# Corner of a triangular inverse: its first copy on VectorE, and one more dense product between it and the products that read it

## The chip, the cores and the metric

The kernel runs on one core of one Trainium2 chip. The metric is the time of one execution in device microseconds, the median of several runs. The engines are called by their names in the profile: PE (TensorE, matmuls), DVE (VectorE), ACT (ScalarE), POOL (GpSimd) and SP (the queue that starts most DMAs).

## What is computed

One layer of a hybrid decoder trunk on a float32 input of 1024 tokens by 1024 channels: a normalised input is projected by one large matrix; three token mixers run on it in parallel; their outputs are gated, merged and projected; a gated feed-forward layer follows. The change lies in the third mixer, whose recurrence runs over all tokens for 8 heads of width 64:

```python
def step(state, inp):
    r_t, d_t, k_t, v_t, kk_t, a_t = inp
    sa = jnp.einsum('bhij,bhj->bhi', state, kk_t)
    state = (state * d_t[..., None, :]
             - sa[..., :, None] * (kk_t * a_t)[..., None, :]
             + v_t[..., :, None] * k_t[..., None, :])
    y_t = jnp.einsum('bhij,bhj->bhi', state, r_t)
    return state, y_t
```

## The kernel before

The recurrence is computed in chunks of 64 tokens. Within a chunk the steps depend on one another through a triangular 64 by 64 matrix, so each chunk of each head needs the inverse of a triangular matrix. Two halves of 32 are inverted on DVE by substitution. The corner that joins them is the product of three 32 by 32 blocks, made on PE in two rounds with a copy from PSUM between them.

`rwkv_branch` treats the mixer in 8 units, each of 4 heads and 256 tokens. They are called units 0 to 7 here. Every unit has three generators:

- `begin` loads the unit's rows and makes its scaled keys. Its steps that matter here: `ps_n` and `sq` (L1137), ln and exp of `sq` on ACT (L1139, L1140), `kap` (L1141), the step that yields 1.5 after `av` (L1145 to L1147), `kb` (L1152, L1153) and `kr` (L1156 and after).
- `finish` makes the chunk matrices A, sends them through DRAM to `N`, inverts (31 rounds of L1247 and L1249, each followed by `yield 0.75`), transposes the result to `XT` (L1254), copies one part to `X22` (L1257, ACT), copies the two diagonal blocks into A (L1266, four on DVE and four on ACT), and then makes the corner. That last part has these steps: 32 small matmuls into `ps_m1` (L1276, called the first products), the copy `M1` out of PSUM (L1277, ACT, 64 partitions by 256), 32 small matmuls into `ps_x12` that read `M1` (L1284, called the second products), and four copies into A (L1287, ACT).
- `chain` carries the state through the unit's chunks in twelve steps. Its tenth step begins with `zp` (L1319, PE) and its copy `zs` (L1321, ACT).

While the chain of unit n runs, `finish` of unit n+1 and `begin` of unit n+2 run beside it. Between their steps the dense products of the large projection fill PE: `fill(1)` issues one piece, which is three products of 512 columns in most places (two high and low parts against each other). There are 448 pieces. The 24 first go beside `begin` of unit 0, the next 48 beside `finish` of unit 0, and each later turn of the loop has 47. A helper class `Steps` says after which piece a step is written: a generator's yields are added up, and a step is written when the sum falls behind the share of pieces done. `finish` is spread by `T_FINISH` over the first 0.93 of a unit's pieces, `begin` by `T_BEGIN` from 0.35 to the end.

That is the order in which the code is written. When the kernel is built, the framework puts each engine's instructions in an order of its own: written order is the preference, but an instruction whose inputs are late by its reckoning is passed by one that is ready. The engines then execute in that fixed order. In the trace, the copy `XT` of a unit often stands ahead of `sq` (L1137) on DVE, though it is written after it.

In the trace, buffer digits are left out of names: `ps_m` is `ps_m1`, `ps_x` is `ps_x12`, `M` is `M1`, `X` is `X` or `X22`, `T` is `T11`. The second products of units 0 to 7 start at 416.87, 461.19, 513.20, 571.51, 627.38, 680.85, 732.60 and 782.21 us.

Of the kernel before, what the change touches and what calls it, by code (L numbers as in the profile page):

```python
# [42 lines left out]
ORDER = "k2k3kkVFqqqquuuuuuuugg"  # L43
LATER = "vvvv"
SLOTS = 12
T_BEGIN, T_FINISH = 25.0, 48.0

PAR_ROWS = [("norm_mix", 8), ("norm_ffn", 8), ("gate_bias", 24), ("c_mu", 14), ("c_w0", 4), ("c_a0", 4),
            ("c_k_k", 4), ("c_k_a", 4), ("c_r_k", 4), ("c_lnx_g", 4), ("c_lnx_b", 4), ("a_ln_g", 8)]
# [984 lines left out]
def rwkv_branch(tc, a, e):  # L1034
    nc = tc.nc
# [3 lines left out]
    with ExitStack() as st:  # L1039
# [40 lines left out]
        ps = mps.tile([P, HALF], F32, name="ps_i", tag="m")  # L1080
# [85 lines left out]
        def finish(n, u):  # L1166
# [52 lines left out]
            ps = mps.tile([P, 4, P], F32, name="ps_v", tag="m")  # L1219
# [6 lines left out]
            for q in range(2):  # L1226
                ps = mps.tile([P, HALF], F32, name="ps_k", tag="m")
# [10 lines left out]
            ps = mps.tile([P, HALF], F32, name="ps_b", tag="m")  # L1238
# [32 lines left out]
            M1 = ch.tile([64, 8, 32], F32, name="M1", tag="M1", bufs=1)  # L1271
            quarters = [slice(32 * v_, 32 * v_ + 32) for v_ in range(2)]
            ps = mps.tile([P, 16, 32], F32, name="ps_m1", tag="m")
            for j in range(8):
                for qs in quarters:
                    nc.tensor.matmul(ps[qs, j, :], NT12[qs, j, :], X22[qs, j, :], start=True, stop=True)  # L1276
            nc.scalar.copy(M1, ps[0:64, 0:8, :])  # L1277
            yield 1.5
            yield 1.0
            pair = [mps.tile([P, 16, 32], F32, name="ps_x12", tag="m") for _ in range(2)]  # L1280
            for j in range(8):
                r0 = 64 * (j % 2)
# [116 lines left out]
        for n in range(-1, 8):  # L1399
            streams = []  # L1400
            if n < 7:
                streams.append(Steps(finish(n + 1, units[n + 1]), T_FINISH, 0.0, 0.93))
            if n < 6:
                streams.append(Steps(begin(n + 2, units[n + 2]), T_BEGIN, 0.35, 1.0))
            body = chain(n, units[n]) if n >= 0 else None
            left = total - sum(lead)
            share = left * (n + 1) // 8 - left * n // 8 if body else lead[1]
            slot = 0
            for p in range(share):
                while body and slot * share <= p * SLOTS and slot < SLOTS:  # L1410
                    next(body)
                    next(last, None)
                    slot += 1
                for s in streams:
                    s.until((p + 1) / share)
                fill(1)
            for s in streams:
                s.rest()
            if body:
                last = body  # L1420
                next(body)
# [181 lines left out]
```

## Time and profile before

| what | us |
| --- | --- |
| median of 3 runs | 2067.66 (2066.97 to 2071.49) |
| the profiled execution | 2057.16 |
| its span, from first to last instruction | 2055.5 |
| stretch with the 8 units, 372 to 800 us of the span: length | 428.00 |
| PE busy in it | 406.94 |
| DVE busy in it | 314.24 |
| ACT busy in it | 213.76 |

A row of the timeline gives start, duration, engine, line of the kernel, operation and shape; in brackets stands how long the engine sat idle before it and what ended that. A row with x2 or more stands for neighbours that were merged. The view of waits gives, for an engine and a line, the total idle time, the number of times and the longest. Releasers are inferred from semaphore events.

### The profile page before, as it was taken

To read this page: it belongs to the slowest core of one execution; us is meant where nothing else is said; L and a number is where in the kernel's file an instruction comes from. 1 tells how busy PE (TensorE), PEld (TensorE's weight loads), DVE (VectorE), ACT (ScalarE), POOL (GpSimd) and SP (SyncE) were. 2 spreads that over 40 slices of the span, in tenths; PEclk is the share of its full clock that TensorE was granted. 3 is DMA by queue.
4 is the path that set the end of the run, shared out by engine and by line. 5 is a ranking of instruction groups with operands and counts; after the bars stand their busy time and mean duration, and the time that the engine had idled before them with its cause. 6 is when DMAs were issued, how large, how long until landed. Compare 5 with 4: busy or idle time off the path is not lost. (4 is left out here: it accounts for less than half of the span.)

```text
span 2055.5 us, 31199 instructions
## 1 busy us (share of the span) xinstructions
PE 1965.8 (96%) x11773; PEld 1581.7 (77%) x11773; DVE 1398.6 (68%) x2798; ACT 921.4 (45%) x1596; POOL 157.3 (8%) x222
## 2 busy tenths in 40 slices
PE   5999999999999999899999899999999999999998
PEld 4788887777877677777766778998788888888886
DVE  7865674868777773365565784458887777756966
ACT  8443335445445654487783122245333332324435
POOL 0000000000000000133232320000000000000000
PEclk9999999989999999899999999999999999999999
DMA  4433335333333322542244852452343233258333
GB/s 134 118 118 118 103 103 186 114 101 112 107 97 111 111 86 73 183 128 59 79 147 162 291 178 89 144 172 65 108 124 123 93 113 103 92 192 302 121 92 128
DMA packets 254698, 260.89 MB, mean 127 GB/s; under 512 B 21430, under 2 KB 195588, under 8 KB 254548
## 3 DMA queue, kind: packets, MB, share of 16 engines
q1 hardware_dynamic: 218964, 210.63, 32.5%
q10 hardware_dynamic: 32352, 39.07, 6.0%
q0 software_dynamic: 3232, 9.21, 1.6%
q8 instruction: 92, 1.51, 0.3%
q14 instruction: 58, 0.48, 0.1%
HBM read 176.77 MB, written 77.89 MB: 124 GB/s over the span
## 5 line engine op out<-in xcount | busy, mean ns | idle before, releaser
L155 PE MATMUL ps_f<-T_hi,o_hi 128*128 128x512 f32 x576 | 227.6, 395 | 6.8 <-ACT o_hi L325 4.3
L157 PE MATMUL ps_f<-T_hi,o_lo 128*128 128x512 f32 x576 | 226.3, 393 | 2.6 <-DVE o_lo L326 2.6
L156 PE MATMUL ps_f<-T_lo,o_hi 128*128 128x512 f32 x576 | 226.9, 394 | 1.0 <-DVE T_lo L326 0.9
L137 ACT CAST w_hi<-w_raw 128x1024 fp32r<-128x1024 f32 (+2 forms) x114 | 112.8, 989 | 177.3 <-PE ps_p L156 51.8
L138 DVE TENSOR_TENSOR w_lo<-w_raw,w_hi 128x1024 fp32r<-128x1024 f32 (+2 forms) x114 | 131.5, 1154 | 70.7 <-ACT w_hi L137 68.7
L155 PEld LDWEIGHTS ps_f<-T_hi,o_hi 128*128 128x128 f32 x576 | 109.3, 190 | 33.6 <-ACT o_hi L325 5.9
L157 PEld LDWEIGHTS ps_f<-T_hi,o_lo 128*128 128x128 f32 x576 | 109.2, 190 | 26.6 <-DVE o_lo L326 3.5
L156 PEld LDWEIGHTS ps_f<-T_lo,o_hi 128*128 128x128 f32 x576 | 109.2, 190 | 25.7 <-DVE T_lo L326 2.3
L325 ACT CAST o_hi<-s 128x512 fp32r<-128x512 f32 x105 | 65.0, 619 | 128.0 <-DVE s L358 50.6
L156 PE MATMUL ps_d<-w_lo,a_hi 128*128 128x512 f32 x272 | 106.7, 392 | 1.7 <-DVE w_lo L977 1.7
L157 PE MATMUL ps_d<-w_hi,a_lo 128*128 128x512 f32 x272 | 106.7, 392 | 0.0
L155 PE MATMUL ps_d<-w_hi,a_hi 128*128 128x512 f32 x272 | 104.7, 392 | 0.0
L901 ACT CAST a_hi<-a_raw 128x1024 fp32r<-128x1024 f32 (+1 forms) x42 | 41.2, 982 | 110.4 <-PE ps_d L156 94.1
L1515 DVE CUSTOM_DVE_ANT_0 lg<-lp,lg 128x128 f32<-128x128 f32 (+7 forms) x64 | 48.0, 756 | 58.1 <-POOL lg L1505 48.7
L326 DVE TENSOR_TENSOR o_lo<-s,o_hi 128x512 fp32r<-128x512 f32 x105 | 72.5, 690 | 18.7 <-PE ps_f L156 11.7
L155 PE MATMUL ps_g<-h_hi,w_hi 128*128 128x512 f32 x192 | 80.0, 417 | 1.0 <-ACT w_hi L137 1.0
L157 PE MATMUL ps_g<-h_hi,w_lo 128*128 128x512 f32 x192 | 75.7, 394 | 0.4 <-DVE w_lo L138 0.4
L156 PE MATMUL ps_o<-w_lo,m_hi 128*128 128x256 f32 x256 | 72.7, 284 | 3.0 <-DVE w_lo L138 3.0
L156 PE MATMUL ps_g<-h_lo,w_hi 128*128 128x512 f32 x192 | 75.4, 393 | 0.0
L628 DVE TENSOR_TENSOR gt<-gt,ps_p 128x512 f32<-128x512 f32 x48 | 32.8, 684 | 60.8 <-PE ps_p L157 60.0
L157 PE MATMUL ps_o<-w_hi,m_lo 128*128 128x256 f32 x256 | 72.4, 283 | 0.0
L902 DVE TENSOR_TENSOR a_lo<-a_raw,a_hi 128x1024 fp32r<-128x1024 f32 (+1 forms) x41 | 47.1, 1149 | 36.9 <-PE ps_d L157 36.0
(488 smaller groups left out, 5457.7 us busy)
## 6 DMA issues: line engine op xcount, KB each, us to landing
w_raw<-in_w_in_dram SPq DMA_DIRECT2D x50, 512.0 KB, 4.1
gt<-gate_d ACTq DMA_DIRECT2D x24, 512.0 KB, 3.9
up_raw<-in_w_gate_up_dram SPq DMA_DIRECT2D x44, 256.0 KB, 3.4
w_raw<-in_w_gate_up_dram SPq DMA_DIRECT2D x22, 512.0 KB, 3.9
a_raw<-act_S SPq DMA_DIRECT2D x20, 512.0 KB, 3.9
w<-in_w_down_dram SPq DMA_DIRECT2D x18, 512.0 KB, 6.2
gate_d<-c SPq DMA_DIRECT2D x33, 256.0 KB, 2.0
w_raw<-in_w_out_dram SPq DMA_DIRECT2D x16, 512.0 KB, 4.3
```

The source lines that it names most:

```text
L137: nc.scalar.copy(hi, raw)
L138: low[0].tensor_tensor(lo, raw, hi.bitcast(F32), ALU.subtract)
L155: nc.tensor.matmul(ps, lhs[0], rhs[0], start=first, stop=False)
L156: nc.tensor.matmul(ps, lhs[0], rhs[1], start=False, stop=False)
L157: nc.tensor.matmul(ps, lhs[1], rhs[0], start=False, stop=last)
L325: nc.scalar.copy(dst[0], src)
L326: eng.tensor_tensor(dst[1], src, dst[0].bitcast(F32), ALU.subtract)
L628: nc.vector.tensor_tensor(gt[:, sl], gt[:, sl], ps, ALU.mult)
L901: nc.scalar.copy(hi, raw)
L902: nc.vector.tensor_tensor(lo, raw, hi.bitcast(F32), ALU.subtract)
L1515: nc.vector.tensor_tensor_reduce(lg[:, 0:nk], lp[:, 0:nk], lg[:, 0:nk], 1.0, NEG, ALU.add, ALU.max, mx)
```

## The change

Three lines change. The copy `M1` is issued on VectorE in place of ScalarE. The second yield after it is 2.5 in place of 1.0. `T_FINISH` is 49.5 in place of 48.0, so the sum of the yields and the number over which they are spread grow by the same amount.

```diff
-T_BEGIN, T_FINISH = 25.0, 48.0
+T_BEGIN, T_FINISH = 25.0, 49.5
...
-            nc.scalar.copy(M1, ps[0:64, 0:8, :])
+            nc.vector.tensor_copy(M1, ps[0:64, 0:8, :])
             yield 1.5
-            yield 1.0
+            yield 2.5
             pair = [mps.tile([P, 16, 32], F32, name="ps_x12", tag="m") for _ in range(2)]
```

By the code's own arithmetic, with 47 pieces for a unit, this is where the steps of `finish` are written in units 1 to 7, counted in pieces (unit 0, with 48, has its first products at 36 before and 35 after, its second ones at 39):

| step | before | after |
| --- | --- | --- |
| first and last round of the substitution | 10, 30 | 10, 30 (some between them one earlier) |
| `XT`, `X22`, `T11` | 33 | 32 |
| diagonal blocks into A | 34 | 33 |
| step of `begin` with L1145 to L1147 | 34 | 34 |
| first products and `M1` | 36 | 35 |
| tenth step of `chain` (`zp`, `zs`) | 36, ahead of the first products | 36 |
| `kb` of `begin` | 36 | 36 |
| second products | 38 | 38 |
| `kr` of `begin` | 38 | 38 |

## The prediction

> **What bounds the kernel now.** I read the page first, then the table by stretches for the 428 us in which the eight units run, then the view of what PE waited for there.
>
> ```profile
> PE 1965.8 (96%) x11773; PEld 1581.7 (77%) x11773; DVE 1398.6 (68%) x2798; ACT 921.4 (45%) x1596; POOL 157.3 (8%) x222
> ```
> ```profile
> 372.00:800.00 428.00, 406.94 (x3932) 318.06 (x3933) 314.24 (x911) 213.76 (x433) 25.78 (x29) 0.97 0.34 101
> ```
> ```profile
> PE ps_x L1284 <- ACT M L1277: 5.7, 4, 2.8
> PE ps_v L1221 <- ACT sq L1364: 3.1, 4, 0.8
> PE ps_r L156 <- DVE w_lo L138: 3.1, 1, 3.1
> ```
>
> PE is the bound: 96% of the whole, and in the stretch 406.94 of 428.00 us (the columns after the length are PE, its weight loads, DVE, ACT, POOL). So a microsecond in which PE does not wait is a microsecond of the kernel, and moves between other engines are worth nothing by themselves. The longest of PE's waits there is the one the change is about: the second products (L1284) wait for the copy M1 (L1277), 5.7 us in 4 of 8 units. That is all that the direct effect can win: 0.28% of 2057. A measurement of this kernel tells about 0.2% (4.1 us) from no change; the three runs before are that far apart.
>
> Why is M1 late? Unit 2 shows it. The first fence is PE, the second ACT and DVE together in order of time.
>
> ```profile
> 508.65 0.45 PE L1319 MATMUL zp<-S,kr 64*64 64x64 f32 x8
> 509.03 0.69 PE L1276 MATMUL ps_m<-X,NT 32*32 32x32 f32 x32
> ...
> 510.46 0.39 PE L155 MATMUL ps_g<-h,w_hi 128*128 128x512 f32 x1
> 510.69 0.40 PE L156 MATMUL ps_g<-h,w_hi 128*128 128x512 f32 x1
> ...
> 513.20 0.45 PE L1284 MATMUL ps_x<-M,T 32*32 32x32 f32 x32 [1.88 <-ACT M L1277]
> ```
> ```profile
> 509.88 1.28 ACT L1140 ACT_TABLE_LOAD   x1
> 511.18 0.63 ACT L1140 ACTIVATE sq<-sq 128x512 f32<-128x512 f32 x1
> 511.84 0.69 DVE L1141 TENSOR_TENSOR kap<-kap,sq 128x512 f32<-128x512 f32 x1 [3.22 <-ACT sq L1140]
> ...
> 512.57 0.74 DVE L1145 TENSOR_SCALAR sq<-av,par,oka 128x256 f32<-128x256 f32 x2
> ...
> 512.79 0.36 ACT L1277 COPY M<-ps_m 64x256 f32<-64x256 f32 x1
> ...
> 513.22 0.68 DVE L1156 TENSOR_TENSOR kr<-kap,pd 128x504 f32<-128x504 f32 x1
> ...
> 515.01 0.68 DVE L1152 TENSOR_TENSOR kb<-k,pi 64x512 f32<-64x512 f32 x1
> ```
>
> The first products are over at 509.72 (509.03 + 0.69), but ACT reaches M1 only at 512.79, 3.07 us later: it is in begin's exp of sq with its table load. PE would have reached the second products at 513.20 - 1.88 = 511.32. DVE is held by the same exp: kap waits 3.22 us for it, and everything queued behind kap waits too. So the question is not whether DVE is quicker at the copy, but on which side of kap the copy is queued.
>
> **The change, part by part.** *The yields.* The second products stay at piece 38; the first ones, with XT and the diagonal copies, go one piece forward, and past the tenth chain step. A piece is three starts 0.23 apart (510.46, 510.69), so 0.69; zp takes 0.38 (508.65 to 509.03). PE thus does the first products about 1.07 us earlier, and reaches the second ones when it did: the third dense piece and zp come out of the time ahead of the first products. The distance grows, but only at its front end. Where M1 is late because its engine is busy, this gives nothing. Its cost: the first products need X22, which has room except in unit 1:
>
> ```profile
> 457.00 0.40 ACT L1257 COPY X<-XT 64x256 f32<-64x256 f32 x1
> ...
> 458.17 0.69 PE L1276 MATMUL ps_m<-X,NT 32*32 32x32 f32 x32
> ...
> 459.38 0.69 DVE L1141 TENSOR_TENSOR kap<-kap,sq 128x512 f32<-128x512 f32 x1 [2.02 <-ACT sq L1140]
> ...
> 461.19 0.45 PE L1284 MATMUL ps_x<-M,T 32*32 32x32 f32 x32 [0.74 <-ACT M L1277]
> 461.44 0.68 DVE L1156 TENSOR_TENSOR kr<-kap,pd 128x504 f32<-128x504 f32 x1
> ...
> 463.24 0.67 DVE L1152 TENSOR_TENSOR kb<-k,pi 64x512 f32<-64x512 f32 x1
> ```
>
> There the first products would come at 458.17 - 1.07 = 457.10, before X22 is done at 457.40: up to 0.4 us of waiting. It is lost only if M1 is then in time; if not, it comes off the later wait. I take nothing. The substitution rounds that go a piece forward add no instruction, and I take nothing for them: each needs the one before it.
>
> *The copy on DVE.* The trace has no such copy. Its nearest row is another DVE copy out of PSUM, as many columns on twice the partitions:
>
> ```profile
> L1544 DVE COPY ob<-op 128x256 f32<-128x256 f32 x16 | 6.7, 421 | 12.4 <-PE op L1541 12.4
> ```
>
> I take 0.42; on ACT it took 0.36, and the two ends move the sum by 0.06 in each of five units, 0.3 us. ACT loses eight copies; nothing that PE waits for stands right behind them but zs of the chain, which stood ahead.
>
> *Where it stands on DVE.* The framework fixes this at build time, and the trace of before has to tell. L1145 to L1147 are written one piece ahead of M1 and kb one behind it. Yet kr, written far later, stands between L1145 and L1146 in units 1, 2, 4, 5 and 6: where L1146 was not ready by the framework's reckoning, whatever was ready went in. In unit 3 that place went to z, an add that is written inside a dense piece near the first products:
>
> ```profile
> 569.40 0.16 DVE L288 TENSOR_TENSOR z<-ps_r,fb 128x8 f32<-128x8 f32 x1
> 569.52 0.69 DVE L1146 TENSOR_TENSOR k<-k,sq 128x512 f32<-128x512 f32 x1
> 570.13 0.68 DVE L1147 SCALAR_TENSOR_TENSOR av<-kap,av 128x512 f32<-128x512 f32 x1
> 570.73 0.68 DVE L1152 TENSOR_TENSOR kb<-k,pi 64x512 f32<-64x512 f32 x1
> 571.51 0.34 PEld L1284 LDWEIGHTS ps_x<-M,T 32*32 32x32 f32 x32
> ```
>
> So I put M1 into that gap, ahead of kr. It then starts where kr starts now, ends 0.42 later, and the second products follow 0.05 later (unit 2: 512.79 + 0.36 = 513.15, start 513.20). The rows of the other units:
>
> ```profile
> 627.22 0.67 DVE L1156 TENSOR_TENSOR kr<-kap,pd 128x504 f32<-128x504 f32 x1
> 627.38 0.34 PEld L1284 LDWEIGHTS ps_x<-M,T 32*32 32x32 f32 x32 [0.36 <-ACT M L1277]
> ...
> 629.02 0.67 DVE L1152 TENSOR_TENSOR kb<-k,pi 64x512 f32<-64x512 f32 x1
> ```
> ```profile
> 678.18 0.69 DVE L1141 TENSOR_TENSOR kap<-kap,sq 128x512 f32<-128x512 f32 x1 [3.22 <-ACT sq L1140]
> ...
> 679.56 0.68 DVE L1156 TENSOR_TENSOR kr<-kap,pd 128x504 f32<-128x504 f32 x1
> ...
> 680.85 0.45 PE L1284 MATMUL ps_x<-M,T 32*32 32x32 f32 x32 [2.84 <-ACT M L1277]
> ...
> 681.36 0.68 DVE L1152 TENSOR_TENSOR kb<-k,pi 64x512 f32<-64x512 f32 x1
> ```
> ```profile
> 730.79 0.69 DVE L1141 TENSOR_TENSOR kap<-kap,sq 128x512 f32<-128x512 f32 x1 [1.23 <-ACT sq L1140]
> ...
> 732.17 0.68 DVE L1156 TENSOR_TENSOR kr<-kap,pd 128x504 f32<-128x504 f32 x1
> ...
> 732.60 0.45 PE L1284 MATMUL ps_x<-M,T 32*32 32x32 f32 x32 [0.22 <-ACT M L1277]
> ...
> 733.97 0.68 DVE L1152 TENSOR_TENSOR kb<-k,pi 64x512 f32<-64x512 f32 x1
> ```
>
> PE's wait becomes the start of kr + 0.47, less the moment at which PE is free (start less wait):
> - unit 1: 461.91 - 460.45 = 1.46 (now 0.74)
> - unit 2: 513.69 - 511.32 = 2.37 (1.88)
> - unit 4: 627.69 - 627.38 = 0.31 (0)
> - unit 5: 680.03 - 678.01 = 2.02 (2.84)
> - unit 6: 732.64 - 732.38 = 0.26 (0.22)
> - unit 3: 569.40 + 0.47 = 569.87, in time for 571.51; units 0 and 7 showed no wait, and unit 7 has no begin beside it. Nothing.
>
> The sum is 6.42 against 5.68: +0.7 us. On the profiled execution (2057.16, of which 2055.5 is span) that is 2057.9; the median stands 10.5 us higher, and there it is 2068.4. What the copy pushes back by about 0.4 us on DVE is kr, L1146, L1147 and kb of a unit that is two behind the chain, and behind them the splits w_lo. PE waited 3.1 us for one w_lo in the whole stretch; 0.4 us there, once, is the bound I keep for that.
>
> **The rivals.** *M1 ahead of kap (win).* DVE is idle for 2.02, 3.22, 3.22 and 1.23 us before kap in units 1, 2, 5 and 6. A copy queued there costs nothing and is done before PE comes: all 5.7 us go, less unit 1's 0.4. Time: 2062. For it: M1's input is now ready 1.07 us earlier, in unit 2 at about 508.6, long before the exp ends. Against it: the framework seems to reckon exp much earlier than it comes (it ordered M1 behind exp on ACT too, though M1's input was there first), and kap comes before M1 in written order.
>
> *M1 behind L1147 (loss).* Written order says so. If M1's input is reckoned ready only after the gap, kr takes the gap, and L1146 and L1147 have preference. M1 then starts where kb starts now. The waits are 463.71 - 460.45 = 3.26, 515.48 - 511.32 = 4.16, 629.49 - 627.38 = 2.11, 681.83 - 678.01 = 3.82 and 734.44 - 732.38 = 2.06; unit 3 (571.20) is still in time. Sum 15.41, so +9.7 us: 2077.4. It decides from the point where M1 stands behind L1146. DVE, busy 314 of 428 us against ACT's 214, is the engine with less room.
>
> The Trainium skill (Perfetto Trace Analysis, Optimizing Scalar/DVE Operations) says that work may be offloaded to Scalar when DVE is saturated; this change goes the other way, and by that rule the result would be this rival's. The trace bears it out in part only: DVE is the busier, but it idles right before kap.
>
> *The distance does not grow.* The framework could leave the first products where they are, if it reckons X22 late. By the above this changes nothing for M1 behind kap, since its input was ready anyway; it belongs to the forecast.
>
> **How the numbers follow.** M1 behind kap, in the gap or directly after kap: 0.45. In the gap it is 2068.4. Directly after kap M1 starts 0.65 earlier (512.57 in place of 513.22), which takes 0.65 off the waits of units 1, 2 and 5 and all of 4 and 6, 2.5 of the 6.42: 2065.9. Own range 2065 to 2071. M1 ahead of kap: 0.27, 2062. M1 behind L1147: 0.18, 2077.4. The framework moves something else as well, either way by a few us: 0.10. Faster by over 0.2%: 0.27 + 0.04 = 0.31. Slower: 0.18 + 0.06 = 0.24. The rest, 0.45, is within 0.2%. The range reaches to both rivals: 2061 to 2077.5.
>
> **What would show it.** Right: on DVE, M1 stands behind kap and L1145 in units 1 to 6; PE's wait L1284 <- DVE M is near 6.4 us in total; three pieces and zp lie between first and second products, whose start has not moved. Wrong: that wait is gone and M1 stands in the idle time before kap (then 2062), or M1 stands behind L1147 and the wait is near 15 us; or PE's other waits change by more than 3 us, which would mean a reordering I have not seen.

## The result, and the profile after

| | median, us | runs | profiled execution | its span |
| --- | --- | --- | --- | --- |
| before | 2067.64 (2063.32 to 2074.52) | 8 | 2057.16 | 2055.5 |
| after | 2081.49 (2074.26 to 2086.84) | 8 | 2083.67 | 2082.0 |

The ratio is 1.0057 (95% interval 1.0040 to 1.0074): slower by 11.8 us, with 8.3 to 15.3 as the interval. It is near the ratio of the two means, which lie 11.9 us apart; the medians in the table lie 13.9 apart. The two profiled executions are further apart, 26.5 us, because that of before lies 10.5 us under its own median. So the two traces are compared stretch by stretch below, and not by their ends.

The line of PE on the page of after, its 428 us with the units, and PE's waits in them:

```profile
PE 1987.9 (95%) x11773; PEld 1595.1 (77%) x11773; DVE 1401.2 (67%) x2806; ACT 918.9 (44%) x1588; POOL 150.7 (7%) x222
```
```profile
372.00:800.00 428.00, 399.57 (x3753) 310.94 (x3754) 315.04 (x914) 200.90 (x405) 19.72 (x29) 0.94 0.33 98
```
```profile
PE ps_x L1284 <- DVE M L1277: 11.7, 4, 3.9
PE ps_v L1221 <- ACT sq L1364: 3.1, 4, 0.8
PE ps_r L156 <- DVE w_lo L138: 3.1, 1, 3.1
```

Two things changed. The wait ahead of the second products went from 5.7 to 11.7 us, while the other two waits stayed as they were. And the granted clock in the stretch (the column after POOL) fell from 0.97 to 0.94. PE is the busiest engine in both kernels, and eight copies moved from ACT to DVE (1596 to 1588, 2798 to 2806), so the page alone says little.

Unit 2 of after, first PE, ACT and DVE in order of time:

```profile
516.63 0.69 PE L1276 MATMUL ps_m<-X,NT 32*32 32x32 f32 x32
...
518.15 0.45 PE L1319 MATMUL zp<-S,kr 64*64 64x64 f32 x8
...
519.82 0.63 ACT L1140 ACTIVATE sq<-sq 128x512 f32<-128x512 f32 x1
...
520.48 0.69 DVE L1141 TENSOR_TENSOR kap<-kap,sq 128x512 f32<-128x512 f32 x1 [3.23 <-ACT sq L1140]
...
521.21 0.74 DVE L1145 TENSOR_SCALAR sq<-av,par,oka 128x256 f32<-128x256 f32 x2
...
521.86 0.68 DVE L1156 TENSOR_TENSOR kr<-kap,pd 128x504 f32<-128x504 f32 x1
...
522.46 0.68 DVE L1146 TENSOR_TENSOR k<-k,sq 128x512 f32<-128x512 f32 x1
...
523.06 0.68 DVE L1147 SCALAR_TENSOR_TENSOR av<-kap,av 128x512 f32<-128x512 f32 x1
...
523.66 0.41 DVE L1277 COPY M<-ps_m 64x256 f32<-64x256 f32 x1
...
524.12 0.65 PE L1284 MATMUL ps_x<-M,T 32*32 32x32 f32 x32 [3.95 <-DVE M L1277]
```

The first products are over at 517.32 (516.63 + 0.69). M1 itself takes 0.41 us, but it stands sixth in a row behind the exp of `begin`: kap, L1145, kr, L1146, L1147, M1. It starts 6.34 us after its input is there, and PE stands for 3.95 us. Units 1 and 6 have another order:

```profile
467.31 0.74 DVE L1145 TENSOR_SCALAR sq<-av,par,oka 128x256 f32<-128x256 f32 x2
...
467.96 0.41 DVE L1277 COPY M<-ps_m 64x256 f32<-64x256 f32 x1
```
```profile
748.92 0.69 DVE L1141 TENSOR_TENSOR kap<-kap,sq 128x512 f32<-128x512 f32 x1 [1.22 <-ACT sq L1140]
749.52 0.41 DVE L1277 COPY M<-ps_m 64x256 f32<-64x256 f32 x1
749.86 0.72 DVE L1145 TENSOR_SCALAR sq<-av,par,oka 128x256 f32<-128x256 f32 x2
```

In unit 1 M1 stands in the gap behind L1145, in unit 6 directly behind kap, and in units 2 to 5 behind L1147. (In unit 3 the gap went to z in place of kr.)

| PE's wait at L1284, us | unit 1 | 2 | 3 | 4 | 5 | 6 | sum |
| --- | --- | --- | --- | --- | --- | --- | --- |
| before | 0.74 | 1.88 | 0 | 0 | 2.84 | 0.22 | 5.7 |
| after | 2.18 | 3.95 | 0 | 1.81 | 3.76 | 0 | 11.7 |

That is 6.0 us of the 11.8. The clock can account for the rest. Four stretches of 10 us that begin shortly before the second products of units 1, 2, 4 and 5 in after, and then those of units 2 and 5 in before (PEclk is the third number from the end):

```profile
466.00:476.00 10.00, 7.82 (x85) 5.57 (x84) 9.45 (x21) 4.20 (x12) 1.77 (x1) 0.83 0.00 0
522.00:532.00 10.00, 7.88 (x87) 6.17 (x87) 6.99 (x13) 3.07 (x8) 0.58 (x1) 0.66 0.06 23
640.00:650.00 10.00, 8.50 (x87) 6.30 (x88) 6.41 (x13) 3.67 (x9) 0.77 (x1) 0.83 0.04 16
695.00:705.00 10.00, 7.61 (x65) 5.68 (x66) 5.89 (x12) 2.63 (x9) 0.57 (x1) 0.66 0.07 26
```
```profile
511.00:521.00 10.00, 8.12 (x95) 6.32 (x94) 8.58 (x17) 5.75 (x15) 2.71 (x1) 0.83 0.14 52
679.00:689.00 10.00, 8.15 (x85) 6.03 (x86) 7.01 (x15) 5.02 (x13) 1.41 (x1) 0.83 0.07 26
```

Inside them the clock is 1.00 or 0.50 and nothing between, so 0.83 means 3.4 us at half speed (0.17 x 2 x 10) and 0.66 means 6.8. After has 3.4 + 6.8 + 3.4 + 6.8 = 20.4 us at half speed right behind these waits; before has 6.8. PE does half its work in the 13.6 us more, which costs up to 6.8. Together 6.0 + 6.8 = 12.8, against 11.8 (8.3 to 15.3) measured.

The two traces bear this out over the whole stretch from the second products of unit 0 to those of unit 7, first before, then after:

```profile
416.87:782.21 365.34, 347.60 (x3484) 271.22 (x3483) 272.08 (x788) 184.17 (x379) 24.74 (x27) 0.97 0.34 100
421.62:800.53 378.91, 355.00 (x3487) 274.65 (x3486) 274.81 (x795) 182.16 (x372) 18.68 (x27) 0.95 0.33 97
```

It is 13.6 us longer. PE's idle time grows by 6.2 (from 17.7 to 23.9), and PE is busy 7.4 us longer with the same products. Of the other 12.9 us between the two spans, 4.8 lie ahead of this stretch and 8.2 behind it. Those behind are not put down to the change: e4 and e9 below, which are faster than before, have as long an end (1281.4 and 1279.5 us, after 1281.4, before 1273.3).

### The profile page after: what moved, and what is told of

It is laid out like the page before. It is cut to its first block, busy times and chain, and to the rows that moved or that the text cites. A ratio compares the mean times of both kernels' runs of the same rounds, so it can differ in the third digit from the quotient of the medians.

```text
span 2082.0 us, 31196 instructions
## 1 busy us (share of the span) xinstructions
PE 1987.9 (95%) x11773; PEld 1595.1 (77%) x11773; DVE 1401.2 (67%) x2806; ACT 918.9 (44%) x1588; POOL 150.7 (7%) x222
## 5 line engine op out<-in xcount | busy, mean ns | idle before, releaser
L155 PE MATMUL ps_o<-w_hi,m_hi 128*128 128x256 f32 x256 | 72.7, 285 | 0.0
```

The lines of the kernel that those rows point to most:

```text
L155: nc.tensor.matmul(ps, lhs[0], rhs[0], start=first, stop=False)
```

## The experiments

Theory Q: the time follows M1's place in its engine's queue, through PE's wait at L1284 and the halved clock behind long waits. Theory R: the shifted steps and the changed order of PE cost the time, and the engine of the copy does not matter. Theory C: the clock drops by chance, and so does the difference.

**The copy alone, and the yields alone.** e1 is before with the copy on VectorE; e2 is after with the copy back on ScalarE.

```diff
 e1, against before
-            nc.scalar.copy(M1, ps[0:64, 0:8, :])
+            nc.vector.tensor_copy(M1, ps[0:64, 0:8, :])
 e2, against before
-T_BEGIN, T_FINISH = 25.0, 48.0
+T_BEGIN, T_FINISH = 25.0, 49.5
...
-            yield 1.0
+            yield 2.5
```

> Only the copy M1 goes to VectorE; both yields and T_FINISH stay as before. Theory Q (M1's place in DVE's queue, and a halved PE clock after each wait of about 2 us): M1 stands behind L1147 in units 1, 2, 4 and 5, PE's wait L1284 <- DVE M is 13 to 14 us in all, and the time is 12 to 16 us over before. Rival R (the shifted steps, one more piece and another order of the products on PE, cost the time): within 3 us of before. Rival C (a clock that differs from run to run by itself, not by these waits): within 3 us of before on the median.

> Yields 1.5 and 2.5 and T_FINISH 49.5 as after; the copy M1 stays on ScalarE. Theory Q: ACT reaches M1 behind the exp as before, PE reaches the second products at the same piece, so the wait L1284 <- ACT M is 5 to 7 us and the time within 3 us of before, though three pieces and zp lie between. Rival R: 9 to 14 us over before, like the full change. Rival C: within 3 us of before.

e1: 2086.31 us against 2069.22, ratio 1.0088 (1.0071 to 1.0105). e2: 2065.1 against 2069.22, ratio 0.9981 (0.9964 to 0.9998). PE's wait of e1, then its unit 2, then the wait of e2:

```profile
PE ps_x L1284 <- DVE M L1277: 14.8, 6, 4.2
```
```profile
519.04 0.69 DVE L1141 TENSOR_TENSOR kap<-kap,sq 128x512 f32<-128x512 f32 x1 [3.22 <-ACT sq L1140]
...
521.62 0.68 DVE L1147 SCALAR_TENSOR_TENSOR av<-kap,av 128x512 f32<-128x512 f32 x1
522.22 0.41 DVE L1277 COPY M<-ps_m 64x256 f32<-64x256 f32 x1
...
522.68 0.65 PE L1284 MATMUL ps_x<-M,T 32*32 32x32 f32 x32 [4.15 <-DVE M L1277]
```
```profile
PE ps_x L1284 <- ACT M L1277: 3.7, 3, 1.5
```

The copy alone costs more than the whole change, and the yields alone cost nothing; they gain about 4 us (0.4 to 7.4). So theory R falls: e2 moves the same steps, and PE's order in it is that of after but for two short places. In e1 M1 stands behind L1147 in unit 2 too. In e2 M1 still stands behind the exp of `begin` on ACT in units 1 to 6, but further forward behind it. Unit 5 shows the most, first before, then e2:

```profile
678.49 1.28 ACT L255 ACT_TABLE_LOAD   x1
...
680.42 0.37 ACT L1277 COPY M<-ps_m 64x256 f32<-64x256 f32 x1
```
```profile
682.59 0.37 ACT L1277 COPY M<-ps_m 64x256 f32<-64x256 f32 x1
682.98 1.28 ACT L255 ACT_TABLE_LOAD   x1
```

Before has a table load of a gate ahead of M1, e2 has it behind, and the wait of this unit falls from 2.84 to 0.85 us (that of unit 1 rises from 0.74 to 1.31). None of e2's three waits is longer than 1.54 us, and no halved clock stands behind any of them.

**M1 ahead of the wait for exp.** e4 is after with a yield of `begin` ahead of `ps_n` raised from 1.0 to 8.0, so that ln, exp and kap (L1139 to L1141) are written later beside `finish`, and M1 stands ahead of kap on DVE in units 1 to 6. e9 is e4 with the copy on ScalarE. e10 is after once more, beside e9.

```diff
 e4, against after (L1134, ahead of ps_n)
-T_BEGIN, T_FINISH = 25.0, 49.5
+T_BEGIN, T_FINISH = 32.0, 49.5
...
-            yield 1.0
+            yield 8.0
 e9, against e4
-            nc.vector.tensor_copy(M1, ps[0:64, 0:8, :])
+            nc.scalar.copy(M1, ps[0:64, 0:8, :])
```

> As after, but the yield ahead of begin's ps_n is 8.0 in place of 1.0 (T_BEGIN 32), so that sq, ln, exp and kap are written later and M1 stands ahead of kap on DVE in units 1 to 7. Theory Q: the wait at L1284 is below 1 us, and the time is 5 to 9 us under before, less whatever begin's delay costs elsewhere (at most 3 us). Rival R: the PE order is that of after or further from before, so 9 to 14 us over before. Rival C: within 3 us of before.

> As e4_m_ahead, with the copy M1 on ScalarE: there it stands between ln and exp of begin, ahead of the exp. Theory Q (the place in the queue, not the engine): M1 is in time or nearly so, the wait at L1284 is below 2 us, and the time is 2 to 7 us under before, like e4. If the engine mattered: back at before or above it.

> The changed kernel once more. Theory Q: the same waits (2.2, 3.9, 1.8 and 3.8 us, within 0.3), each followed by a halved clock; 8 to 15 us over before. The halved stretches elsewhere in its first profile (one at 373 us, several behind 810 us), if they belong to the run and not to the change, come in other places or lengths.

e4: 2062.92 against 2069.22, ratio 0.9971 (0.9957 to 0.9986). e9: 2064.25 against 2067.31, 0.9985 (0.9971 to 0.9998). e10: 2080.97 against 2067.31, 1.0061 (1.0039 to 1.0082). Unit 2 of e4 and its waits, and the wait of e10:

```profile
508.31 0.69 PE L1276 MATMUL ps_m<-X,NT 32*32 32x32 f32 x32
...
509.22 0.41 DVE L1277 COPY M<-ps_m 64x256 f32<-64x256 f32 x1
...
511.80 0.45 PE L1284 MATMUL ps_x<-M,T 32*32 32x32 f32 x32
...
513.12 0.69 DVE L1141 TENSOR_TENSOR kap<-kap,sq 128x512 f32<-128x512 f32 x1 [3.50 <-ACT sq L1140]
```
```profile
PE ps_r L156 <- DVE w_lo L138: 5.9, 2, 3.1
...
PE zp L1319 <- DVE S L1340: 2.5, 2, 1.9
```
```profile
PE ps_x L1284 <- DVE M L1277: 11.8, 4, 3.9
```

Here M1 follows its products by 0.22 us (508.31 + 0.69 = 509.00 to 509.22), and kap still waits 3.50 us for exp, but with M1 ahead of it and nobody harmed. With the same copy on the same engine the time is 18 us under that of after (0.9971 against 1.0057, of 2068). e9 gains as well, so the engine is not the point; whether DVE is better by some 3 us there is open, since the intervals overlap. e10 gives after's time and after's waits again. It also has as much half speed between 440 and 800 us, 23.9 us in both profiled executions. So theory C falls too: the clock drops at the same four waits again, and the intervals of after, e1 and e10 lie clear of 1. It falls by these intervals: that the two traces have the same 23.9 us is partly luck, as the last section shows. Not all of the direct gain arrives in e4. All 5.7 us at L1284 are gone, but the waits for w_lo rose from 3.1 to 5.9 and two waits of 2.5 us in all came at zp.

**The second products later.** If the wait costs the time, moving only its end should take the cost away. e3 is before with the second yield 4.5 in place of 1.0; e5 is after with 4.7 in place of 2.5; e6 and e7 are e1 with 4.5 and 2.1 in place of 1.0; e8 is e2 with 4.7 in place of 2.5.

```diff
 e3, against before (e5 to e8 change this yield alone, each in its own kernel)
-            yield 1.0
+            yield 4.5
```

> M1 on ScalarE and T_FINISH 48 as before; the second yield is 4.5 in place of 1.0, so only the second products go back by three pieces (five between in place of two). Theory Q: PE no longer waits at L1284 (5.7 us gone, and the halved clock behind two of these waits, 3 us more): 6 to 9 us under before. Rival R: no gain, or a loss, since the order on PE changes in every unit. Rival C: within 3 us of before.

> As after, but the second yield is 4.7 in place of 2.5: M1 stays where after has it on DVE (behind L1147 in units 2 to 5), and the second products come two pieces and one chain step later. Theory Q (M1's place in DVE's queue against the moment PE asks for it, and a halved PE clock after waits of about 1.8 us and more): the waits of 2.2, 3.9, 1.8 and 3.8 us shrink by about 1.9 us each, to 4 us in all, at most two of them long enough to halve the clock; 2 to 6 us under before, so 14 us or more under after. Rival R (the order of the products on PE and the shifted steps cost the time): still 8 us or more over before.

> As e1_dve_only, but the second yield is 4.5 in place of 1.0: the second products come three pieces and one chain step later. Theory Q: the waits of about 4 us shrink by 2.5 us each to 1.2 to 1.7 us, 4 to 5 us in all, none followed by a halved clock; within 5 us under to 1 us over before. If the copy on DVE were dear by itself (what it delays on DVE), 8 us or more over before.

> As e1_dve_only, but the second yield is 2.1 in place of 1.0: one piece later. Theory Q: each wait shrinks by 0.7 us: 3.3, 3.5, 1.3 and 3.4 us, 11.5 in all, three of them followed by a halved clock: 11 to 15 us over before, 3 to 7 under e1. Rival R: no different from e1.

> As e2_space_only (M1 on ScalarE, first products one piece forward), with the second yield 4.7 in place of 2.5. Theory Q: no wait at L1284 is left; 4 to 8 us under before, if the wait for w_lo at the first row block (3.4 us in e3) does not come up again; with it 2 to 5 us under.

| | copy | wait at L1284, us | half speed in 440 to 800 us, us | median and that of before, us | ratio (95%) |
| --- | --- | --- | --- | --- | --- |
| before | ACT | 5.7 | 10.2 | | |
| after | DVE | 11.7 | 23.9 | 2081.49, 2067.64 | 1.0057 (1.0040 to 1.0074) |
| e10 | DVE | 11.8 | 23.9 | 2080.97, 2067.31 | 1.0061 (1.0039 to 1.0082) |
| e1 | DVE | 14.8 | 30.6 | 2086.31, 2069.22 | 1.0088 (1.0071 to 1.0105) |
| e7 | DVE | 11.6 | 17.1 | 2073.33, 2067.06 | 1.0032 (1.0018 to 1.0045) |
| e5 | DVE | 3.2 | 13.7 | 2065.6, 2067.06 | 0.9997 (0.9981 to 1.0013) |
| e6 | DVE | 2.8 | 6.9 | 2067.16, 2067.06 | 1.0003 (0.9990 to 1.0016) |
| e2 | ACT | 3.7 | 10.2 | 2065.1, 2069.22 | 0.9981 (0.9964 to 0.9998) |
| e3 | ACT | 0 | 6.8 | 2064.67, 2069.22 | 0.9984 (0.9967 to 1.0001) |
| e8 | ACT | 0 | 3.4 | 2067.05, 2067.06 | 0.9996 (0.9981 to 1.0011) |
| e4 | DVE | 0 | 13.6 | 2062.92, 2069.22 | 0.9971 (0.9957 to 0.9986) |
| e9 | ACT | 0.4 | 6.8 | 2064.25, 2067.31 | 0.9985 (0.9971 to 0.9998) |

The half speed is added up from stretches of 5 us in the one profiled execution of each kernel (0.50 for 5 us counts 5); it leaves out unit 0, where every kernel has 3 to 14 us of it between 405 and 440 us, and the time behind 800 us, with 36 to 60. One of e7's twelve runs took 3294 us; the median and the ratio do not feel it.

With 11.6 us of wait or more the kernel is slower, with 5.7 or less it is not; nothing lies between. e7 tells wait and clock apart as far as these runs can: its wait is after's (11.6), its halved clock 6.8 us shorter, and it costs 6.6 us in place of 11.8. In its trace PE is busy 352.0 us between the second products of units 0 and 7, 3.0 less than in after. The halved time is that of one execution, though, and the 6.6 us are those of eleven. e5 shows the same for after itself: M1 stands where it stood, only its reader comes later, and the loss is gone. The rows of e5, e6 and e7:

```profile
PE ps_x L1284 <- DVE M L1277: 3.2, 3, 2.1
```
```profile
PE ps_x L1284 <- DVE M L1277: 2.8, 2, 1.6
```
```profile
PE ps_x L1284 <- DVE M L1277: 11.6, 4, 3.5
```

Missed: the gain below 5.7 us of wait. Without any wait at L1284 e3 gains about 3 us, which is not clear of zero (its interval reaches 1.0001), and e8 nothing, though several us were expected of both; e5 does not gain the 2 to 6 us expected either. The losses were missed too: e1 costs 18 us where 12 to 16 were expected, and e7 6.6 where 11 to 15 were. And e2 has 3.7 us of wait, where 5 to 7 were expected. The traces show new waits at other places, first e3, the splits w_lo and the chain, then e8:

```profile
PE ps_r L156 <- DVE w_lo L138: 6.5, 2, 3.4
...
PE us L1327 <- ACT zs L1321: 1.5, 1, 1.5
```
```profile
PE ps_r L156 <- DVE w_lo L138: 5.2, 2, 3.1
...
PE us L1327 <- ACT zs L1321: 2.1, 2, 1.7
```

In e3 it is one split, queued on DVE until begin's work is done, and PE needs its result at once:

```profile
519.99 1.22 DVE L138 TENSOR_TENSOR w_lo<-w_raw,w_hi 128x1024 fp32r<-128x1024 f32 x1
...
521.26 0.58 PE L156 MATMUL ps_r<-w_lo,h_hi 128*128 128x256 f32 x1 [3.42 <-DVE w_lo L138]
```

When PE comes sooner, it meets w_lo too early: 3.4 us of the 5.7 go there, and PE's clock is halved for 6.8 us from 519.9 on, during this wait and behind it. That this accounts for all of e8's missing gain was not shown.

## Why the prediction was wrong

Its number was 2068.4 with a range of 2061 to 2077.5; the median is 2081.49. The time came out on the side of its slower rival, and beyond that rival's 2077.4.

- **Right: what bounds the kernel, the copy's price, the order of PE.** PE's waits are what counts. M1 takes 0.41 on DVE, where 0.42 was estimated. Between first and second products lie three pieces and zp. The question was indeed "on which side of kap the copy is queued": e4 has it ahead and wins. PE's other waits in the stretch did not change.
- **The step that failed: "So I put M1 into that gap, ahead of kr."** It holds in unit 1 alone (in unit 6 M1 is directly behind kap, which the forecast also counted as its own). In units 2 to 5 kr or z kept the gap, and M1 went behind L1147, as the slower rival had it. The argument was that whatever was ready took the gap, with z of unit 3 as the example. But z and kr were themselves candidates for it, and one place takes one instruction. What was not asked is where M1 stands among several that could be reckoned ready. Begin's step with L1145 to L1147 is written one piece ahead of M1, and the trace of after has this written order in four of six units.
- **Mis-sized: the slower rival's +9.7.** It placed M1 behind L1147 in five waiting units; two of them, 1 and 6, came out otherwise. So its 15.41 us of waits became 11.7, +6.0 in place of +9.7. In units 2, 4 and 5 its waits were near: 4.16, 2.11 and 3.82, measured 3.95, 1.81 and 3.76.
- **Left out of every case: the clock.** Each microsecond of waiting was priced at one microsecond. The trace of before already had PE at half speed for 3.4 us behind its waits of 1.88 and 2.84, and not behind those of 0.74 and 0.22. Had this been read, the slower rival's waits of 3.26, 4.16, 2.11, 3.82 and 2.06 would each have got at least 3.4 us at half speed: 17.0 less 6.8, of which half is lost, some 5 us more: 2082.5. That this lies 1 us from the median is partly luck: the rival's waits are 3.7 us too long, and after has more halved clock than this.
- **The yields.** They were put at nothing; alone they gain about 4 us (e2), and with the copy on DVE they save about 6 (1.0057 in place of 1.0088, whose intervals just meet). "Where M1 is late because its engine is busy, this gives nothing" was wrong: earlier first products changed M1's place in its engine's order. In e2 it got ahead of the gate's table load in unit 5, while the prediction had read only begin's exp in unit 2 as the cause; in after it got ahead of L1146 in unit 1, where e1 has it behind L1147 (2.18 us of wait in place of 3.99).

The Trainium skill's rule (Perfetto Trace Analysis, Optimizing Scalar/DVE Operations), with which the prediction had paired the slower rival, gave the right sign here. Its reason, that DVE is the fuller engine, is not what decided: with DVE just as full, e4 wins.

What stays open: how much of the 11.8 us is wait and how much clock. No experiment kept the waits and took all the halved clock away. The split 6.0 and up to 6.8 is worked out from the traces (6.2 idle and 7.4 longer busy over units 0 to 7); e7 is the nearest test of it. Its excess waits, 5.9, with half of its 3.4 us more behind them, 1.7, make 7.6, and 6.6 was measured. For e1 the same sum is 9.1 + 6.8 = 15.9, and 18.2 was measured (ratio 1.0088 of 2069.22); its trace is 17.5 us longer than before's between the second products of units 0 and 7, 9.6 of it idle and 7.9 busy. Why the framework put M1 directly behind kap in unit 6 and behind L1147 in unit 2 was not looked into.

## What to carry to other kernels

Before moving a short operation to another engine, look up what will stand ahead of it there, in the order that is built: if an instruction in that queue waits microseconds for a third engine, the copy waits with it, and 0.41 us of work cost 18 us alone (e1). Where the order has the copy behind such a waiting instruction, delay the waiting work or the reader of the copy by some pieces (e4, e5), rather than change the engine. And price a wait of the bounding engine with the clock that may be halved behind it.

## What the runs showed of the hardware

A wait of PE of under 2 us can halve its clock. Over units 1 to 6 of before, after, e1, e2, e5, e6, e7 and e10, all 18 waits at L1284 of 1.81 us or more had PE at 0.50 within the wait or right behind it, for 3.4 us or twice that; of 12 shorter ones (0.20 to 1.59 us), only one did, the longest. The same products behind such a wait in before and in e2, where the waits are 1.88 and 1.54 us:

```profile
514.40:516.47 2.07, 2.07 (x21) 1.20 (x19) 2.06 (x5) 0.36 (x2) 2.07 (x1) 0.50 0.00 0
515.68:516.88 1.20, 1.20 (x21) 0.72 (x19) 1.20 (x3) 0.38 (x2) 1.20 (x1) 1.00 0.00 0
```

PE counts as busy all through in both, but the same 21 products take 2.07 us in the one and 1.20 in the other: a busy PE is not a fast PE.

Elsewhere it is less regular: of 17 waits for w_lo of 2.1 to 3.4 us between 440 and 800 us of the twelve traces, four had no halved clock behind them. The halved stretches of a trace begin on a raster of 3.41 us (in before at 514.35, 558.73 and 681.61, which are 13 and 36 such steps apart), and what counts is how long PE idles within one step of it. PE was idle for 1.78 us or more in 32 of the steps at full speed between 440 and 800 us, and the next step was at 0.50 all 32 times; of the 1191 other such steps 5 were followed by one (1.41 to 1.59 us idle), and none of the four with 1.65 to 1.69. So the same wait for w_lo, 3.07 us in before and 3.06 in e3, halves the clock in the one, where 2.90 us of idling lie in one step, and not in the other, where it is cut into 1.41 and 1.65:

```profile
555.29:558.70 3.41, 0.51 (x4) 0.51 (x5) 3.06 (x13) 1.09 (x3) 0.00 (x0) 1.00 0.23 77
```
```profile
557.45:560.86 3.41, 2.00 (x31) 1.72 (x29) 2.96 (x14) 1.93 (x5) 0.00 (x0) 1.00 0.22 74
560.86:564.28 3.42, 1.77 (x17) 1.63 (x17) 3.22 (x9) 0.00 (x0) 0.00 (x0) 1.00 0.17 40
```

Where the raster lies against the code differs from trace to trace (in after and e10 by 0.3 us only), so whether a wait of 2 to 3 us also halves the clock is partly luck, and that holds for the waits near 2 us at L1284 too.

The Trainium skill (TensorE: Matmul & The Clock Gate, Part 1: The HAM clock gate) has the half-speed state follow at least one idle window of about 3.4 us. The steps of 3.4 us agree with that; but PE need not be idle for a whole one, since 1.8 us of idling in a step were enough here.

The halved stretches elsewhere in the traces (between 370 and 390 us in after, e5, e6, e8 and e10, between 405 and 440 us in all twelve) and those behind 800 us come in kernels that are no slower than before as well as in slower ones, so they are not put down to the change.
